# Attention's output kept by features, its squares read from PSUM: a hybrid diffusion layer on one core

## The chip, the core and the metric

One core of a Trainium2 chip runs the whole layer as one program. The metric is the device time of an execution in microseconds; "before" is the median of three runs. The core's engines each work through a queue of their own, in order: TensorE (PE, with its weight loads shown as PEld), VectorE (DVE), ScalarE (ACT), GpSimd (POOL), and SyncE (SP), which here only issues DMA transfers. They wait for one another by semaphores. TensorE writes its results into PSUM, a memory of eight banks, each with 512 fp32 columns on 128 partitions.

## The reference, cut to what matters

The layer serves 256 prompt tokens and 2048 latent tokens, width 1024. Its first half computes differential attention for four heads, and Fourier mixing beside it; both are joined by one output projection.

```python
s = einsum('bqhmd,bkhmd->bhmqk', q, k) * scale      # two maps m per head
p = softmax(s, axis=-1)
a = p[:, :, 0] - lam * p[:, :, 1]
o = einsum('bhqk,bkhe->bqhe', a, v)                 # 128 features e per head
...
a = rms_norm(o, subln_g) * (1.0 - lam_init)         # over the 128 features of a head
mix = concatenate([a.reshape(b, n, 512), four], axis=-1) @ w_out
```

The RMS norm of a head's output needs, for each query, the sum of squares over that head's 128 features, and one factor per query. Prompt tokens attend to themselves (256 keys), latent tokens to 512 cached and 2048 latent keys. A squared-ReLU MLP follows.

## The kernel before, in words

The kernel works in stages, one behind the other: modulation, input projection, Fourier mixing, attention, output projection with its norm, and two MLP stages that multiply by Strassen-like sums. The change touches attention and the output projection.

**Attention.** The work is cut into groups: 256 queries of one head make a group of two tiles (j = 0, 1), 8 groups a head, 32 in all, and one prompt group per head beside them. No loop order decides what runs when: every step of a group is entered in a list `ev` with a time in units of u (one unit is 5.2 / 5 us, five units make a step T), the list is sorted, and each engine's queue gets its instructions in that order. A step's time is thus a place in the queues, not a promise. A group takes 20 units. Seen from the start G of a group's period:

- The scores of a tile and a map (`fill`, L1080, 2 x 5 matmuls of 512 keys) go to five PSUM banks `S`; DVE takes their maxima (`rowmax`, L1085), ACT exponentiates them from there (`exp`, L1104, at 0, 5, 10 and 15 units, five each). The scores of the next map are written into the same five banks as they come free.
- POOL joins the two maps (`combine`, L1111 to L1120).
- PE transposes the result block by block (`tr`, L1135, two banks `pt`), ACT and DVE split it into a high and a low part (`ah` L1142, `al` L1147), and PE multiplies by the values (`mul`, L94 to L96, at 3.9, 8.9, 13.9 and 18.9 units; two of ten blocks in full precision, L1161). The products are summed in columns 0 to 255 of one bank, `po`, which holds features by queries: 128 features on the partitions, 256 queries.
- Behind a group's last product come the steps `o1` to `o6`: ACT copies the sum to SBUF (`oT`, L1172, 6 units into the next group's period), PE turns it into columns 256 to 511 of the same bank (`o2`, L1176, 6.4), DVE copies that out to `o` (`o3`, L1180, 10.25), ACT squares the copy with a running sum, one instruction for each tile (`o4`, L1186, 14.5), DVE adds epsilon (`o5`, L1189, 15.2) and POOL takes the power -1/2 (L91), POOL scales `o` and SP stores it (`o6`, L1195 and L1196, 15.6) as queries by features into `att`.

The bank `po` is shared: the prompt group's scores, and its products (`mul`, L1246, in two calls at 15.4 and 17.0 units), also lie in its columns 256 to 511, at times when no sample group's output is there. Its `o3` (L1250) copies them out; its `o4` to `o6` come about a group later.

For the last group the steps behind `o1` are not in the list but in `LASTO`, which the output projection interleaves with its first matmuls; their store runs on POOL's queue.

**Output projection.** 18 tiles of 128 tokens, each 2 x 24 matmuls (`out_mm`). Per tile SP loads `att` (L1560) and the Fourier half (L1562, by features already); `mix` has PE turn the attention half (L1572, four transposes), ACT copy it out with the gain (L1573), and DVE split it into high and low parts (L1576, L1577). Tile 0 is turned within the attention stage (`mix0_tr`, `mix0_copy`, L1280 and L1283). The output weights are split on the way in (`w_split`, L1544 and L1545).

Of the kernel before, what the change touches and what calls it, by code (L numbers as in the profile page):

```python
# [41 lines left out]
def body(tc, a, out):  # L42
    nc = tc.nc
    ctx = ExitStack()
    with ctx:
# [16 lines left out]
        att = [scratch(f"att{i}", [P, 512]) for i in range(NT // P)]  # L62
# [46 lines left out]
        def setup_cond(pool, pps, rows):  # L109
# [8 lines left out]
            nc.vector.tensor_scalar_mul(cols[:, 96:97], cols[:, 96:97], 1.0 - LAM_INIT)  # L118
# [870 lines left out]
        with ExitStack() as c3_:  # L989
# [49 lines left out]
            class Group:  # L1039
# [66 lines left out]
                def combine(self, j):  # L1106
# [5 lines left out]
                    nc.gpsimd.tensor_scalar(self.s0e[:, j:j + 1], tot[:, 0:1], tot[:, 0:1], EPS, op0=ALU.mult, op1=ALU.mult)  # L1112
# [65 lines left out]
                def o3(self):  # L1178
                    self.o = self.op.tile([P, 256], F32, tag="o", name=f"o{self.nm}")
                    nc.vector.tensor_copy(self.o, self.po[:, 256:512])  # L1180

                def o4(self):
                    osq = self.op.tile([P, P], F32, tag="osq", name=f"osq{self.nm}", bufs=1)
                    self.oss = self.op.tile([P, 4], F32, tag="oss", name=f"oss{self.nm}")
                    for j in range(2):
                        nc.scalar.activation(osq, self.o[:, j * P:j * P + P], AF.Square, accum_out=self.oss[:, j:j + 1])  # L1186

                def o5(self):
                    nc.vector.scalar_tensor_tensor(self.oss[:, 0:2], self.oss[:, 0:2], 1.0 / P, self.s0e, op0=ALU.mult, op1=ALU.add)  # L1189
                    pow_mhalf(self.oss[:, 2:4], self.oss[:, 0:2], 2)  # L1190

                def o6(self):
                    for j in range(2):
                        c = slice(j * P, j * P + P)
                        nc.gpsimd.tensor_scalar(self.o[:, c], self.o[:, c], self.oss[:, 2 + j:3 + j], 0.0, op0=ALU.mult, op1=ALU.add)  # L1195
                        (nc.gpsimd if self.last else nc.sync).dma_start(att[self.hd.tok0 + self.g * 2 + j][:, self.hd.hc], self.o[:, c])  # L1196

            class Prompt(Group):
# [21 lines left out]
                def combine(self, j):  # L1220
# [3 lines left out]
                    nc.gpsimd.tensor_scalar(self.s0e[:, j:j + 1], t[:, 2:3], t[:, 2:3], EPS, op0=ALU.mult, op1=ALU.mult)  # L1224
# [13 lines left out]
                def mul(self, j):  # L1238

                    (ah, al), V = self.A[0], self.hd.V  # L1240
                    n = 0
                    for t in range(2):
                        c = slice((t * 2 + j) * P, (t * 2 + j) * P + P)
                        for l, r in ((ah[:, c], V[:, t, 0, :]), (ah[:, c], V[:, t, 1, :]), (al[:, c], V[:, t, 0, :])):
                            n += 1
                            nc.tensor.matmul(PRO()[:, 256 + j * P:256 + j * P + P], l, r, start=False, stop=(n == 6), skip_group_check=True)  # L1246

                def o3(self):
                    self.o = self.op.tile([P, 256], F32, tag="o", name=f"o{self.nm}")
                    nc.vector.tensor_copy(self.o, PRO()[:, 256:512])  # L1250


# [8 lines left out]
            def load_wout():  # L1261
# [9 lines left out]
                MIX0.extend((f32(ts[0])[:, 2 * D:2 * D + 512], f32(ts[2])[:, 4 * D:5 * D].rearrange("p (k t) -> p k t", t=P)))  # L1271
                nc.sync.dma_start(MIX0[1][:, 4:8, :], four[:, 0:P].rearrange("(k p) t -> p k t", p=P))

            def mix0_load():
                nc.sync.dma_start(MIX0[0], att[0])

            def mix0_tr(gr):
                MIX0.append(gr.bank("pmx0", "pt"))
                for k in range(4):
                    nc.tensor.transpose(MIX0[2][:, k * P:k * P + P], MIX0[0][:, k * P:k * P + P], ident)  # L1280

            def mix0_copy():
# [849 lines left out]
```

## Time and profile before

| what | before |
|---|---|
| runs, median (lowest to highest) | 2862.73 us (2862.22 to 2862.76) |
| the profiled execution, span from the first to the last instruction | 2861.4 us |
| mean granted TensorE clock | 0.999 |
| DVE / ACT / POOL busy, whole span | 71% / 54% / 38% |
| DMA, mean | 172 GB/s |

Three kinds of lines are used below. A line of the timeline gives the start of an instruction, or of several alike in a row, in microseconds from the span's start, then the microseconds to the end of the last of them, engine, line of the kernel, operation, what it writes and reads, shapes, and a count; a bracket at the end is the idle time of that engine just before and who ended it. A line of groups gives a count behind the shape, and behind the bar the busy time, the mean duration in ns, and the idle time before. A line of the waits reads: who waited, for whom, microseconds in total, how often, the longest. A matmul's end is that of its pipeline: the next one starts before it, so that the step from start to start is what it costs PE.

### The profile page before, as it was taken

How to read it: one execution, taken by the hardware profiler on the slowest of the kernel's cores; microseconds unless marked ns; L12 is line 12 of the kernel's file. 1: busy time of each engine (PE TensorE's matmuls, PEld its weight loads, DVE VectorE, ACT ScalarE, POOL GpSimd, SP SyncE). 2: the span in 40 equal slices, each digit the busy share in tenths (PEclk: the TensorE clock that was granted, in tenths of full speed). 3: DMA queues.
4: the chain of work that ended last, by engine and by line, in shares of the span. 5: the costliest groups of instructions: out<-in, count | busy, mean ns of one | idle time of the engine just before them, and what ended most of it. 6: DMA issues, size and time to landing. Idle time of an engine off the chain costs nothing.

```text
span 2861.4 us, 43224 instructions
## 1 busy us (share of the span) xinstructions
PE 2831.7 (99%) x15109; PEld 2455.9 (86%) x15109; DVE 2018.0 (71%) x3393; ACT 1548.2 (54%) x3505; POOL 1073.3 (38%) x890
## 2 busy tenths in 40 slices
PE   8999999999999999999999999999999999999999
PEld 5888888688888888888889999999998888888887
DVE  7767886898988989864477777778775354345554
ACT  4333323798989989853356565556555332333221
POOL 1211223798999989942223333333332000000000
PEclk9999999999999999999999999999999999999999
DMA  7776777421211212036767676667747464445663
GB/s 284 219 207 198 230 213 237 172 106 38 73 71 53 106 38 99 23 124 201 242 221 232 223 246 228 221 219 238 234 167 255 147 202 135 138 144 185 206 206 111
DMA packets 392780, 492.94 MB, mean 172 GB/s; under 512 B 26467, under 2 KB 306384, under 8 KB 389490
## 3 DMA queue, kind: packets, MB, share of 16 engines
q1 hardware_dynamic: 387136, 479.73, 50.9%
q0 software_dynamic: 1872, 7.28, 0.8%
q10 hardware_dynamic: 3554, 3.17, 0.4%
q8 instruction: 119, 1.95, 0.3%
q14 instruction: 99, 0.81, 0.1%
HBM read 312.58 MB, written 179.59 MB: 172 GB/s over the span
## 4 chain that ended last, share of the span: by engine, by line
PE 54%; DVE 1%; DMA 0%; ACT 0%; issue 0%; SPq 0%; POOL 0%; DVEq 0%; POOLq 0%
PE ps L94 8%; PE ps L95 8%; PE ps L96 8%; PE pB L1749 2%; PE pB L1747 2%; PE pB L1748 2%; PE pA L1748 2%; PE pC L1748 2%; PE pA L1749 2%; PE pC L1747 2%; PE pA L1747 2%; PE pC L1749 2%; PE po L94 2%; PE po L96 2%; PE po L95 2%; PE pD L1749 1%
## 5 line engine op out<-in xcount | busy, mean ns | idle before, releaser
L1085 DVE TENSOR_REDUCE mxs<-Ss 128x1 f32<-128x512 f32 x636 | 405.4, 686 | 65.5 <-PE Ss L1080 55.1
L1420 DVE TENSOR_TENSOR sl<-sr,sh 128x768 fp32r<-128x768 f32 x168 | 161.8, 964 | 331.5 <-ACT sh L1419 331.1
L1120 POOL TENSOR_TENSOR P0s<-P0s,P1s 128x1024 f32<-128x1024 f32 (+2 forms) x128 | 378.6, 2958 | 10.7
L1419 ACT CAST sh<-sr 128x768 fp32r<-128x768 f32 x168 | 140.6, 838 | 418.3 <-PE ps L95 418.3
L1789 POOL TENSOR_TENSOR gs<-g,g 128x384 f32<-128x384 f32 x48 | 69.7, 1452 | 468.5 <-ACT g L1759 418.9
L1104 ACT ACTIVATE P1s<-Ss,mxs 128x512 f32<-128x512 f32 x318 | 215.4, 694 | 36.3 <-DVE mxs L1088 35.3
L94 PE MATMUL pj<-wh,hh 128*128 128x512 f32 x576 | 228.8, 397 | 2.0 <-DVE hh L555 2.0
L94 PE MATMUL ps<-thT,sh 128*128 128x512 f32 x585 | 227.6, 389 | 0.0
L95 PE MATMUL ps<-tlT,sh 128*128 128x512 f32 x585 | 227.6, 389 | 0.0
L96 PE MATMUL ps<-thT,sl 128*128 128x512 f32 x585 | 227.6, 389 | 0.0
L95 PE MATMUL pj<-wl,hh 128*128 128x512 f32 x576 | 227.1, 394 | 0.5 <-DVE wl L516 0.5
L96 PE MATMUL pj<-wh,hl 128*128 128x512 f32 x576 | 225.6, 392 | 0.0
L1104 ACT ACTIVATE P0s<-Ss,mxs 128x512 f32<-128x512 f32 x318 | 214.3, 691 | 5.6 <-DVE mxs L1088 5.0
L1135 PE MATMUL pts<-ident,P0s 128*128 128x128 f32 x1280 | 191.7, 273 | 4.5 <-DVE als L1147 1.8
L1080 PE MATMUL Ss<-KS0s,Qs 128*128 128x512 f32 x636 | 190.1, 419 | 0.4 <-ACT P1s L1104 0.4
L1080 PE MATMUL Ss<-KS1s,Qs 128*128 128x512 f32 x636 | 188.7, 420 | 1.5 <-ACT P0s L1104 1.4
L1758 ACT ACTIVATE g<-uz 128x384 f32<-128x384 f32 x144 | 75.7, 526 | 200.2 <-DVE uz L1781 174.1
L1135 PEld LDWEIGHTS pts<-ident,P0s 128*128 128x128 f32 x1280 | 151.3, 140 | 35.9 <-issue 4.8
L1119 POOL TENSOR_SCALAR P1s<-P1s,tots 128x1024 f32<-128x1024 f32 (+2 forms) x128 | 171.9, 1343 | 5.8
L1147 DVE TENSOR_TENSOR als<-pts,ahs 128x512 fp32r<-128x512 f32 x256 | 165.9, 681 | 6.9 <-ACT ahs L1142 6.7
L94 PE MATMUL ps<-ophT,sh 128*128 128x512 f32 x423 | 164.7, 389 | 1.1 <-DVE uz L1781 1.1
L96 PE MATMUL ps<-ophT,sl 128*128 128x512 f32 x423 | 164.6, 389 | 0.0
(536 smaller groups left out, 8073.9 us busy)
## 6 DMA issues: line engine op xcount, KB each, us to landing
sr<-sd SPq DMA_DIRECT2D x84, 768.0 KB, 4.5
a<-in_w SPq DMA_DIRECT2D x184, 256.0 KB, 4.2
sd<-gs SPq DMA_DIRECT2D x192, 192.0 KB, 1.9
sd<-g SPq DMA_DIRECT2D x144, 192.0 KB, 2.1
wm<-in_w_mod SPq DMA_DIRECT2D x32, 512.0 KB, 5.2
Qs<-qd SPq DMA_DIRECT2D x32, 512.0 KB, 4.0
b<-in_w SPq DMA_DIRECT2D x64, 256.0 KB, 5.8
b<-tsum SPq DMA_DIRECT2D x64, 256.0 KB, 4.7
```

The lines of the kernel that those rows point to most:

```text
L94: nc.tensor.matmul(ps, lh, rh, start=first, stop=False)
L95: nc.tensor.matmul(ps, lh, rl, start=False, stop=False)
L96: nc.tensor.matmul(ps, ll, rh, start=False, stop=last)
L1080: nc.tensor.matmul(S[:, :w], self.Q[:, x, m, j * P:j * P + P], self.hd.KS[m][:, b * 512:b * 512 + w], start=(x == 0), stop=(x == 1))
L1085: nc.vector.tensor_reduce(self.mx[j][:, m, b:b + 1], self.S[j, m, b], axis=AX.X, op=ALU.max)
L1104: nc.scalar.activation(dst, S, AF.Exp, bias=self.mx[j][:, m, 6:7], accum_out=self.sm[j][:, m, b:b + 1])
L1119: nc.gpsimd.tensor_scalar(p, p, tot[:, 3:4], 0.0, op0=ALU.mult, op1=ALU.add)
L1120: nc.gpsimd.tensor_add(d, d, p)
L1135: nc.tensor.transpose(pt[:, c:c + P], self.p0[j][:, (kb + t) * P:(kb + t + 1) * P], ident)
L1747: nc.tensor.matmul(ps, wh[:, c], hh[:, k, :], start=first and k == 0, stop=False, skip_group_check=True)
L1748: nc.tensor.matmul(ps, wh[:, c], hl[:, k, :], start=False, stop=False, skip_group_check=True)
L1749: nc.tensor.matmul(ps, wl[:, c], hh[:, k, :], start=False, stop=k == 3, skip_group_check=True)
```

## The change

It does six things. The output stays as features by queries (`oT`), and that is what is scaled and stored; the turned form stays in PSUM and serves the sums of squares alone, which ACT reads there (`o4`), so `o3` and the tile `o` are gone. Epsilon is added on POOL instead of DVE, and the division by 128 moves into epsilon and into the gain. The 256 factors of a group, which lie on the partitions of the queries, are stored to DRAM (`o6`) and loaded back broadcast over all partitions (`o7`); POOL multiplies (`o8`), and one store writes the group (`o9`). The prompt's product has V as the stationary operand, so it comes out by features too, and gets a turn in a `pt` bank of its own. In the projection, `mix_load` loads the attention half by features, the four transposes and ACT's copy go, and the gain moves into the first four blocks of the output weights.

```diff
-        att = [scratch(f"att{i}", [P, 512]) for i in range(NT // P)]
+        att = [scratch(f"att{i}", [512, 2 * P]) for i in range(NT // 256)]
+        rsd = [scratch(f"rs{h}", [NT // 256, 256]) for h in range(H)]
...
                 def o1(self):
-                    self.oT = self.op.tile([P, 256], F32, tag="oT", name=f"oT{self.nm}", bufs=1 if self.last else 2)
+                    self.oT = self.op.tile([P, 256], F32, tag="oT", name=f"oT{self.nm}", bufs=1 if self.last else 3)
...
-                def o3(self):
-                    self.o = self.op.tile([P, 256], F32, tag="o", name=f"o{self.nm}")
-                    nc.vector.tensor_copy(self.o, self.po[:, 256:512])
                 def o4(self):
...
-                        nc.scalar.activation(osq, self.o[:, j * P:j * P + P], AF.Square, accum_out=self.oss[:, j:j + 1])
+                        nc.scalar.activation(osq, self.po[:, 256 + j * P:256 + j * P + P], AF.Square, accum_out=self.oss[:, j:j + 1])
                 def o5(self):
-                    nc.vector.scalar_tensor_tensor(self.oss[:, 0:2], self.oss[:, 0:2], 1.0 / P, self.s0e, op0=ALU.mult, op1=ALU.add)
+                    nc.gpsimd.tensor_add(self.oss[:, 0:2], self.oss[:, 0:2], self.s0e)
                     pow_mhalf(self.oss[:, 2:4], self.oss[:, 0:2], 2)
+                def place(self):
+                    return nc.gpsimd if self.last else nc.sync, self.hd.tok0 // 2 + self.g
                 def o6(self):
-                    for j in range(2):
-                        c = slice(j * P, j * P + P)
-                        nc.gpsimd.tensor_scalar(self.o[:, c], self.o[:, c], self.oss[:, 2 + j:3 + j], 0.0, op0=ALU.mult, op1=ALU.add)
-                        (nc.gpsimd if self.last else nc.sync).dma_start(att[self.hd.tok0 + self.g * 2 + j][:, self.hd.hc], self.o[:, c])
+                    q, n = self.place()
+                    q.dma_start(rsd[self.hd.h][n].rearrange("(p j) -> p j", j=2), self.oss[:, 2:4])
+                def o7(self):
+                    q, n = self.place()
+                    self.rb = self.op.tile([P, 256], F32, tag="P0_1" if self.hd.s else "rb", ...)
+                    q.dma_start(self.rb, rsd[self.hd.h][n:n + 1].partition_broadcast(P).rearrange("p o d -> p (o d)"))
+                def o8(self):
+                    v = self.oT.rearrange("p (j t) -> p j t", j=2)
+                    nc.gpsimd.tensor_mul(v, v, self.rb.rearrange("p (t j) -> p j t", j=2))
+                def o9(self):
+                    q, n = self.place()
+                    q.dma_start(att[n][self.hd.hc], self.oT)
...
+                        for n, (l, r) in enumerate(((0, ah), (1, ah), (0, al))):        # Prompt.mul
+                            nc.tensor.matmul(PRO()[:, 256:512], V[:, t, l, :], r[:, c], ...)
...
-                for t, fn, *args in (... (15.4, gp.mul, 0), (17.0, gp.mul, 1),
-                                     (20.85, gp.o3), (39.5, gp.o4), (40.2, gp.o5), (40.6, gp.o6)):
+                for t, fn, *args in (... (17.0, gp.mul), (20.85, gp.o1), (24.2, gp.o2),
+                                     (24.9, gp.o4), (25.6, gp.o5), (28.2, gp.o6), (32.7, gp.o7),
+                                     (40.2, gp.o8), (43.0, gp.o9)):
...
-                    for t, fn in ((0, gr.o1), (0.4, gr.o2), (0.75 if gr.last else 4.25, gr.o3), (8.5, gr.o4), (9.2, gr.o5), (9.6, gr.o6)):
-                        if gr.last and t:
+                    for t, fn in ((0, gr.o1), (0.4, gr.o2), (8.5, gr.o4), (9.2, gr.o5), (11.8, gr.o6), (16.3, gr.o7), (23.4, gr.o8), (26.0, gr.o9)):
+                        if gr.last and t > 1:
...
-                    nc.scalar.copy(wh[k], WOUT[k][:, c])
-                    nc.vector.tensor_sub(wl[k], WOUT[k][:, c], f32(wh[k]))
+                    if k < H:
+                        nc.scalar.activation(wh[k], WOUT[k][:, c], AF.Copy, scale=cols[:, 96:97])
+                        nc.vector.scalar_tensor_tensor(wl[k], WOUT[k][:, c], cols[:, 96:97], f32(wh[k]), op0=ALU.mult, op1=ALU.subtract)
...
             def mix_load(i):
-                nc.sync.dma_start(am, att[i])
+                nc.sync.dma_start(mT[:, 0:4, :], att[i // 2][:, c:c + P].rearrange("(k p) t -> p k t", p=P))
...
-                    for k in range(4):
-                        nc.tensor.transpose(pm[:, k, :], am[:, k * P:k * P + P], ident)
-                    nc.scalar.activation(mT[:, 0:4, :], pm, AF.Copy, scale=cols[:, 96:97])
```

In the list the times of the prompt's steps count from the start of the head's sixth group period, so 24.2 is 4.2 units into the seventh. The times of the sample groups' `o` steps count from 6 units into the period that follows the group's products: 8.5 is at 14.5.

More of the change, by code (lines that the diff above doesn't have):

```diff
@@ L1236, in al, with mul, o1, o2 @@
                     self.A[0].append(t)
-                def mul(self, j):
+                def mul(self):
                     (ah, al), V = self.A[0], self.hd.V
-                    n = 0
                     for t in range(2):
[L1243 to L1250, printed above, removed]
+                        c = slice(t * 256, t * 256 + 256)
+                        for n, (l, r) in enumerate(((0, ah), (1, ah), (0, al))):
+                            nc.tensor.matmul(PRO()[:, 256:512], V[:, t, l, :], r[:, c], start=False, stop=(t == 1 and n == 2), skip_group_check=True)
+                def o1(self):
+                    self.oT = f32(at.tile([P, 512], F32R, tag="ahp", name=f"oT{self.nm}", bufs=1))[:, 0:256]
+                    nc.scalar.copy(self.oT, PRO()[:, 256:512])
+                def o2(self):
+                    self.pt[1] = pT.tile([P, 512], F32, tag="pt", name=f"pt{self.nm}_o")[:, 0:256]
+                    for j in range(2):
+                        nc.tensor.transpose(self.pt[1][:, j * P:j * P + P], self.oT[:, j * P:j * P + P], ident)
+                def o4(self):
+                    osq = at.tile([P, P], F32, tag="osq", name=f"osq{self.nm}", bufs=1)
+                    self.oss = at.tile([P, 4], F32, tag="oss", name=f"oss{self.nm}")
+                    for j in range(2):
+                        nc.scalar.activation(osq, self.pt[1][:, j * P:j * P + P], AF.Square, accum_out=self.oss[:, j:j + 1])
             ev = []
```

42 lines of the change are left out of this document (17 added, 25 removed).

## The prediction

> **What bounds the kernel now.** I read the page first, then the busy time by stretches, then who waited for whom in the attention stage, then PE's and ACT's instructions in order of time. The page says whose time the span is:
>
> ```profile
> span 2861.4 us, 43224 instructions
> PE 2831.7 (99%) x15109; PEld 2455.9 (86%) x15109; DVE 2018.0 (71%) x3393; ACT 1548.2 (54%) x3505; POOL 1073.3 (38%) x890
> ```
>
> The stretches show that this holds in both stages which the change touches: the first lies in attention, the second in the output projection. Columns: PE, PEld, DVE, ACT, POOL busy, granted clock, DMA share, GB/s.
>
> ```profile
> 900.00:1000.00 100.00, 100.00 (x651) 85.22 (x649) 89.78 (x179) 91.68 (x256) 92.51 (x74) 1.00 0.26 94
> 1300.00:1400.00 100.00, 100.00 (x491) 83.81 (x490) 49.49 (x65) 37.11 (x88) 27.73 (x25) 1.00 0.65 205
> ```
>
> So an instruction taken from PE is time won, one taken from DVE or ACT is not, and whatever makes PE wait is time lost. In attention the other engines stand at about 90%, so the question there is whether PE still finds its inputs ready. It is closest to ACT: the score matmuls write into five PSUM banks, and each bank is free only when ACT has exponentiated the scores before.
>
> ```profile
> PEld Ss L1080 <- ACT P0s L1104: 16.9, 52, 0.4
> ```
>
> Those 52 waits of PE's weight loads are short, 0.4 us at the longest; PE runs directly behind ACT. An ACT that comes two microseconds late is felt by PE at once.
>
> **Part one: the transposes that go.** In the projection, each tile of the mixed output had four transposes (L1572), and tile 0 had four in attention (L1280).
>
> ```profile
> L1572 PE MATMUL po<-ident,am 128*128 128x128 f32 x68 | 10.2, 272 | 0.0
> L1280 PE MATMUL pmx<-ident,wout 128*128 128x128 f32 x4 | 0.6, 272 | 0.0
> ```
>
> The busy column counts the tail of the pipeline; what they cost is the step from one start to the next:
>
> ```profile
> 1350.70 0.39 PE L96 MATMUL po<-woh,ml 128*128 128x512 f32 x1
> 1350.93 0.60 PE L1572 MATMUL po<-ident,am 128*128 128x128 f32 x4
> 1351.37 1.04 PE L248 MATMUL ptb<-ident,xn 128*128 128x128 f32 x8
> ```
>
> 1351.37 - 1350.93 = 0.44 us for four; 72 / 4 = 18 sets, so **-7.9 us**. ACT's copy of them and the DVE cast behind it start earlier; neither is on the path. In their place the load must be there: it takes the form of the load of the Fourier half, and is issued a whole tile ahead.
>
> ```profile
> mT<-four SPq DMA_DIRECT2D x17, 256.0 KB, 3.4
> att<-os SPq DMA_DIRECT2D x62, 64.0 KB, 1.6
> ```
>
> A tile takes 2 x 24 matmuls of 0.23 us (1350.70 to 1350.93), over 11 us, against 3.4 us to landing: hidden. If it were not, the term would be gone.
>
> **Part two: the prompt's product.** Twelve 128-wide matmuls in two calls become six 256-wide ones, plus two transposes.
>
> ```profile
> 1209.48 0.33 PE L1246 MATMUL po<-Vp,ahp 128*128 128x128 f32 x2
> ...
> 1210.09 0.68 PE L1080 MATMUL Ss<-KS0s,Qs 128*128 128x512 f32 x2
> ```
>
> One call cost 0.61 us, two 1.2. A 256-wide matmul steps by 0.11 us (1005.93 to 1006.04, quoted below), so six are 0.7; the transposes step by 0.1 each (0.44 / 4), together 0.2. That is -0.3 us for each of four heads, **-1.2 us**.
>
> **Part three: ScalarE reads the squares from PSUM.** This decides. Before, DVE copied the turned output out (o3), and ACT squared the copy (o4) at 8.5 units of the schedule behind o1. Now o4 keeps its place and reads the second half of bank po itself. The first half of that bank is the accumulator of the next group. In the event list, three products of the next group (13.9 units from its start, L1161 and L94 to L96) stand just ahead of o4 (14.5), and the five exponentials of the next scores (15.0 on) just behind it. Here is that place on PE and, below, on ACT:
>
> ```profile
> 1003.77 1.02 PE L1161 MATMUL po<-ahs,vf4s 128*128 128x256 f32 x4
> ...
> 1005.93 0.28 PE L96 MATMUL po<-ahs,Vs 128*128 128x256 f32 x1
> 1006.04 0.60 PE L1135 MATMUL pts<-ident,P0s 128*128 128x128 f32 x4
> 1006.40 1.63 PE L1080 MATMUL Ss<-KS0s,Qs 128*128 128x512 f32 x6
> ...
> 1009.25 0.60 PE L1135 MATMUL pts<-ident,P0s 128*128 128x128 f32 x4
> ```
>
> ```profile
> 1003.93 0.35 ACT L1186 ACTIVATE osqs<-os 128x128 f32<-128x128 f32 x1
> ...
> 1004.63 0.19 ACT L1186 ACTIVATION_READ_ACCUMULATOR osqs<-os 128x1 f32 x1
> 1005.08 0.69 ACT L1104 ACTIVATE P1s<-Ss,mxs 128x512 f32<-128x512 f32 x1 [0.27 <-DVE mxs L1088]
> ...
> 1005.76 0.68 ACT L1104 ACTIVATE P1s<-Ss,mxs 128x512 f32<-128x512 f32 x1
> ...
> 1009.88 0.59 ACT L1142 CAST ahs<-pts 128x512 fp32r<-128x512 f32 x1 [0.38 <-PE pts L1135]
> ```
>
> ACT starts its squares 0.16 us after PE starts the three products. Does a read of the second half wait for writes into the first? The trace shows the reverse case, a write into the first half that waits for a read of the second:
>
> ```profile
> 1237.49 1.10 PE L1161 MATMUL po<-ahs,vf4s 128*128 128x256 f32 x4 [0.56 <-DVE os L1180]
> 1236.92 0.42 DVE L1180 COPY os<-po 128x256 f32<-128x256 f32 x1 [0.72 <-DMA att<-os]
> ```
>
> PE's product goes to columns 0 to 255, DVE's copy reads 256 to 511, and still PE started only when the copy had ended (1236.92 + 0.42 = 1237.34). Order is kept by the bank, not by the column. I take it to hold for reads behind writes too. The Trainium skill says so outright (page "PSUM — Partial Sum Buffer", section "PSUM bank collisions raise a hardware error"): accesses of two engines to one bank and the same 32 partitions have to be kept apart by semaphores, whatever the addresses. By that rule the sum is the forecast; by addresses it would be the first rival below. The trace agrees for the one direction, with the 0.56 us; no row shows the other.
>
> Then o4 waits until the products end, 1005.93 + 0.28 = 1006.21. A wait of ACT on PE is over 0.03 us behind PE's end (1009.25 + 0.60 against 1009.88), and o4 takes 1004.63 + 0.19 - 1003.93 = 0.89. The exponentials start at 1007.13 instead of 1005.08, so the first bank is free at 1007.13 + 0.69 = 1007.82. PE wants it at 1006.40: **1.4 us idle**. Then the next two score products wait for exponentials that come every 0.68 us, while PE needs only 0.45 (two matmuls of 0.23): 0.2 us each, 0.4. A following stretch of the same group gives some back, since ACT is then late by a little less than PE, and the short waits quoted at the start go: -0.25 us, an estimate. About **1.65 us a group**; ends: 1.2 (the first wait less the rebate) and 2.0 (all waits, a 0.2 us hand-over, no rebate).
>
> ```profile
> L1186 ACT ACTIVATE osqs<-os x64: 309/312/358, 580.7 to 1248.9; 128x128 f32<-128x128 f32 x64
> ```
>
> 64 squares are 32 groups. The last three groups' squares have no exponentials behind them; 29 x 1.65 = **+47.9 us** (35 to 58).
>
> The prompt's squares get a true dependency as well: its transposes stand at 4.2 units of a group (behind three products, 3.9) and its o4 at 4.9, ahead of exponentials at 5.0.
>
> ```profile
> 862.42 0.60 PE L1135 MATMUL pts<-ident,P0s 128*128 128x128 f32 x4
> 862.77 0.71 PE L1080 MATMUL Ss<-KS0s,Qs 128*128 128x512 f32 x2
> 863.46 0.44 PE L1176 MATMUL po<-ident,oTs 128*128 128x128 f32 x2
> 861.69 0.69 ACT L1104 ACTIVATE P1s<-Ss,mxs 128x512 f32<-128x512 f32 x1 [0.99 <-DVE mxs L1088]
> ```
>
> PE reaches that place at 862.42 and needs 0.44 us (as the pair at 863.46); o4 then runs 862.9 to 863.8, and the exponentials that began at 861.69 begin 2.1 us later. Less what the inserted transposes take and a like rebate, PE loses 1.7 us a head: **+6.8 us** (3 to 8).
>
> **Part four: the rest.** The DVE copy that made PE wait in the drain goes: 0.56 us, twice, **-1.1**. In the drain o4 also waits for products, then the casts behind it and, at the seam, the last group's transposes are moved ahead, so that PE may wait for o1: **+2.0** (0 to 4), by the nearest wait there, the 0.56, and by o4's delay of 2.2 (1006.21 - 1003.93, rounded down). DVE loses o3 and o5 in every group; PE does not wait for DVE, so nothing. POOL swaps two scalings for one product of 128x256 and a small addition:
>
> ```profile
> L1195 POOL TENSOR_SCALAR os<-os,osss x64: 363/372/1367, 588.6 to 1254.5; 128x128 f32<-128x128 f32 x64
> 599.21 0.26 POOL L1224 TENSOR_SCALAR s0ep<-tlp 128x1 f32<-128x1 f32 x1
> 600.13 0.74 POOL L1226 TENSOR_TENSOR P0p<-P0p,P1p 128x256 f32<-128x256 f32 x1
> ```
>
> -2 x 0.37 + 0.74 + 0.26 (0.7 at most, nearer the small one since the addition has two elements a lane): +0.3 us a group of 22 us, where POOL idles 7.5%, 1.6 us. Hidden; if the cover were gone, the part beyond 1.6 us would be PE's. On SP, the store of the factors (o6) waits for POOL, and the broadcast load (o7) waits in the same queue until it has landed, 1.6 us by the row of the stores above; queued behind is the next group's query load, used three steps of 5.2 us later. o8 stands 11.6 units behind o6, and POOL has a whole combination of the next scores in between, so it finds the factors there. In the last group these run on POOL's queue in the projection, where POOL idles 72%. The scaling of the output weights changes an operand of eight casts and eight subtractions, not their number, and DVE idles half of that stage. None of this is on the path.
>
> **The sum.** -7.9 - 1.2 + 47.9 + 6.8 - 1.1 + 2.0 = +46.5 on the span of 2861.4: 2907.9. The median of the runs shown is 2862.73, 1.3 us above the span, so **2909 us**. Ends: -7.9 - 1.2 - 1.1 with 35 + 3 + 0 gives 2890, with 58 + 8 + 4 gives 2923.
>
> **Rivals.** (1) Not slower: reads are ordered by address, and only the prompt's squares wait. Then the 47.9 goes, and so does the drain's half of the 2.0: 2862.7 - 7.9 - 1.2 - 1.1 + 6.8 + 1 = 2860, no measurable change (0.2%, 5.7 us, is about what a measurement of this kernel tells from none). Against it stands PE's 0.56 us wait; for it, that no row shows a read waiting. It is decided by one thing: whether o4 starts before or after 1006.21 in such a group. (2) Faster: as (1), and PE gets to the prompt's transposes before ACT wants them, where the scheduler puts them ahead of the products. 2860 - 7 = 2853. For it: PE's transposes need only an early ACT copy. Against: elsewhere in the stage both queues follow the event list. (3) GpSimd becomes the bound, reads being ordered by address: if its product reads the interleaved factors so slowly that it costs 2.4 us more, 0.8 us a group is uncovered, 29 x 0.8 = 23: 2883. Point of decision: 1.6 us of added work. The 0.74 row speaks against it.
>
> **How the numbers follow.** Forecast 0.81; rival (1) 0.07, (2) 0.08, (3) 0.04. Ends of the forecast's terms rarely come together, so 2890 to 2923 leaves out little of the 0.81, and the rest lies below. Widened by a microsecond it is 2889 to 2924. Slower 0.85 (forecast and (3)), same 0.07, faster 0.08.
>
> **What would show it.** Right: ACT's squares preceded by an idle time of about 2 us released by PE's L96, and PE's score matmuls by about 1.4 us released by ACT, in 29 groups; PE's busy share in attention near 93%; period of a group from 22 to 23.7 us; the projection shorter by 7.5 us. Wrong: o4 running while L94 to L96 run, attention as long as before, or POOL as the releaser of PE.

## The result and the profile after

| | before | after |
|---|---|---|
| median (lowest to highest) | 2862.73 us (2862.22 to 2863.09) | 2910.35 us (2909.51 to 2911.3) |
| span of the profiled execution | 2861.4 us | 2907.7 us |
| attention, first to last full-precision product | 684.7 us | 737.8 us |
| from there to the end | 1618.2 us | 1613.1 us |
| ordinary group's period in attention | 22.0 us | 23.74 us |

An ordinary period, here and below, is the median over the samples' groups, from one turn of the output to the next in PE's timeline, without the three periods of a head that carry a prompt's products, turn and squares and without the drain, the last two.

The ratio of the times is 1.0168 (95% interval 1.0155 to 1.0180): slower, and 1.4 us from the forecast. The page of the kernel after shows that PE is still the engine of the span, with fewer matmuls (15021 for 15109) and yet 10 us more of busy time, since the tail of a row ahead of a wait and a wait inside a row (2.07 us for six matmuls, below) count as busy:

```profile
span 2907.7 us, 42986 instructions
PE 2841.9 (98%) x15021; PEld 2446.2 (84%) x15021; DVE 1983.5 (68%) x3321; ACT 1535.3 (53%) x3491; POOL 1074.3 (37%) x891
```

The same two stretches by engine as in the prediction (the second 50 us later): in attention every engine has become less busy at once, PE from 100.00 to 95.64, while in the projection PE is as busy as before.

```profile
900.00:1000.00 100.00, 95.64 (x601) 78.29 (x600) 80.99 (x157) 84.66 (x238) 84.87 (x68) 1.00 0.28 71
1350.00:1450.00 100.00, 100.00 (x479) 83.64 (x478) 47.62 (x70) 35.06 (x88) 25.71 (x26) 1.00 0.73 217
```

All engines less busy, none fuller: that is a longer chain of waits, not a heavier engine. To place it, cut the span at the first and the last full-precision product, in the timeline of PE. Before, first, with two neighbouring turns of the output (L1176), whose distance is a group's period:

```profile
558.50 0.38 PE L1161 MATMUL po<-ahs,vf4s 128*128 128x256 f32 x1
...
951.74 0.44 PE L1176 MATMUL po<-ident,oTs 128*128 128x128 f32 x2
973.79 0.44 PE L1176 MATMUL po<-ident,oTs 128*128 128x128 f32 x2
...
1243.20 0.28 PE L1161 MATMUL po<-ahs,vf14s 128*128 128x128 f32 x1
```

And after, with what lies between the three products and the next scores of one group (the lines are one or two further down in this kernel: products L95 to L97 and L1162, scores L1081, transposes L1136, turn L1177, squares L1183, exps L1105):

```profile
556.78 0.38 PE L1162 MATMUL po<-ahs,vf4s 128*128 128x256 f32 x1
...
812.31 0.44 PE L1177 MATMUL po<-ident,oTs 128*128 128x128 f32 x2
...
820.28 1.02 PE L1162 MATMUL po<-ahs,vf4s 128*128 128x256 f32 x4
...
822.39 0.28 PE L97 MATMUL po<-ahs,Vs 128*128 128x256 f32 x1
822.51 0.60 PE L1136 MATMUL pts<-ident,P0s 128*128 128x128 f32 x4
824.20 2.07 PE L1081 MATMUL Ss<-KS0s,Qs 128*128 128x512 f32 x6 [1.09 <-ACT P1s L1105]
...
836.03 0.44 PE L1177 MATMUL po<-ident,oTs 128*128 128x128 f32 x2
...
1294.59 0.28 PE L1162 MATMUL po<-ahs,vf14s 128*128 128x128 f32 x1
```

Attention grew by 737.8 - 684.7 = 53.1 us, what follows shrank by 5.1 (2861.4 - 1243.20 = 1618.2 against 2907.7 - 1294.59 = 1613.1), and the stages ahead were 1.7 shorter in this execution: 53.1 - 5.1 - 1.7 = 46.3, the whole difference of the spans. The change adds no work to the stages ahead, and over the profiled runs of this document, whatever the kernel, their end lies between 556.55 and 558.50 us, so the 1.7 are not put down to it. Within the group, the scores start 824.20 - 820.28 = 3.92 us behind the products; before it was 1006.40 - 1003.77 = 2.63. Six of them then take 2.07 us instead of 1.63. That is 1.29 + 0.44 = 1.73 us, and the periods shown grew from 22.05 to 836.03 - 812.31 = 23.72, by 1.67. ACT's timeline shows what they waited for, in the same group; the first lines are those of a prompt's squares:

```profile
687.67 1.10 ACT L1143 CAST ahs<-pts 128x512 fp32r<-128x512 f32 x2
691.22 0.28 ACT L1271 ACTIVATE osqp<-ptp_o 128x128 f32<-128x128 f32 x1 [2.45 <-issue]
...
819.51 1.09 ACT L1143 CAST ahs<-pts 128x512 fp32r<-128x512 f32 x2
822.71 0.28 ACT L1183 ACTIVATE osqs<-po 128x128 f32<-128x128 f32 x1 [2.11 <-PE po L97]
...
823.28 0.19 ACT L1183 ACTIVATION_READ_ACCUMULATOR osqs<-po 128x1 f32 x1
823.37 0.68 ACT L1105 ACTIVATE P1s<-Ss,mxs 128x512 f32<-128x512 f32 x1
```

ACT stands idle for 2.11 us, starts 0.04 us behind the end of the last product (822.39 + 0.28 = 822.67), and the exponentials start only behind the squares, at 823.37. They could have gone before: DVE had the last of their maxima at 821.50.

```profile
821.34 0.16 DVE L1089 TENSOR_REDUCE mxs<-mxs 128x1 f32<-128x5 f32 x1
```

The waits over all of attention say that it is so in 30 of the 32 groups (who, for whom, us in total, times, longest):

```profile
PEld Ss L1081 <- ACT P1s L1105: 68.6, 116, 1.5
ACT osqs L1183 <- PE po L97: 64.0, 30, 2.3
...
PE Ss L1081 <- ACT P1s L1105: 34.7, 32, 1.2
...
PEld Ss L1081 <- ACT P0s L1105: 14.9, 43, 0.5
...
ACT osqp L1271 <- issue: 9.1, 4, 2.5
```

Thirty waits of the squares on L97, 2.1 us each, four of the prompts' squares, and PE's score matmuls released by ACT. POOL releases PE nowhere.

### The profile page after: what moved, and what is told of

Its sections match the earlier page's. It is cut to its first block, busy times and chain, and to the rows that moved or that the text cites. A ratio compares the mean times of both kernels' runs of the same rounds, so it can differ in the third digit from the quotient of the medians.

```text
span 2907.7 us, 42986 instructions
## 1 busy us (share of the span) xinstructions
PE 2841.9 (98%) x15021; PEld 2446.2 (84%) x15021; DVE 1983.5 (68%) x3321; ACT 1535.3 (53%) x3491; POOL 1074.3 (37%) x891
## 4 chain that ended last, share of the span: by engine, by line
PE 53%; DVE 1%; DMA 0%; issue 0%; ACT 0%; POOL 0%; SPq 0%; DVEq 0%; POOLq 0%
PE ps L95 8%; PE ps L96 8%; PE ps L97 8%; PE pB L1755 2%; PE pB L1753 2%; PE pB L1754 2%; PE pA L1753 2%; PE pA L1754 2%; PE pC L1755 2%; PE pC L1753 2%; PE pA L1755 2%; PE pC L1754 2%; PE po L97 2%; PE po L95 2%; PE po L96 2%; PE pD L1755 1%
## 5 line engine op out<-in xcount | busy, mean ns | idle before, releaser
L1081 PE MATMUL Ss<-KS0s,Qs 128*128 128x512 f32 x636 | 201.6, 429 | 35.1 <-ACT P1s L1105 35.1
L95 PE MATMUL pj<-wh,hh 128*128 128x512 f32 x576 | 228.3, 396 | 2.3 <-DVE hh L556 2.0
L1105 ACT ACTIVATE P1s<-Ss,mxs 128x512 f32<-128x512 f32 x318 | 215.0, 696 | 25.5 <-DVE mxs L1089 24.5
L95 PE MATMUL ps<-thT,sh 128*128 128x512 f32 x585 | 227.6, 389 | 0.0
L97 PE MATMUL ps<-thT,sl 128*128 128x512 f32 x585 | 227.6, 389 | 0.0
L97 PE MATMUL pj<-wh,hl 128*128 128x512 f32 x576 | 225.5, 392 | 0.0
L1105 ACT ACTIVATE P0s<-Ss,mxs 128x512 f32<-128x512 f32 x318 | 214.3, 691 | 5.1 <-DVE mxs L1089 4.0
L1136 PE MATMUL pts<-ident,P0s 128*128 128x128 f32 x1280 | 191.6, 273 | 5.1 <-DVE als L1148 2.0
L1081 PE MATMUL Ss<-KS1s,Qs 128*128 128x512 f32 x636 | 187.9, 419 | 1.8 <-ACT P0s L1105 1.4
L1136 PEld LDWEIGHTS pts<-ident,P0s 128*128 128x128 f32 x1280 | 151.2, 140 | 36.9 <-issue 4.6
L1081 PEld LDWEIGHTS Ss<-KS0s,Qs 128*128 128x128 f32 x636 | 97.6, 189 | 82.9 <-ACT P1s L1105 71.4
L95 PE MATMUL ps<-ophT,sh 128*128 128x512 f32 x423 | 164.7, 389 | 1.1 <-DVE uz L1787 1.1
```

What stands on the lines that cost most here:

```text
L95: nc.tensor.matmul(ps, lh, rh, start=first, stop=False)
L97: nc.tensor.matmul(ps, ll, rh, start=False, stop=last)
L1081: nc.tensor.matmul(S[:, :w], self.Q[:, x, m, j * P:j * P + P], self.hd.KS[m][:, b * 512:b * 512 + w], start=(x == 0), stop=(x == 1))
L1105: nc.scalar.activation(dst, S, AF.Exp, bias=self.mx[j][:, m, 6:7], accum_out=self.sm[j][:, m, b:b + 1])
L1136: nc.tensor.transpose(pt[:, c:c + P], self.p0[j][:, (kb + t) * P:(kb + t + 1) * P], ident)
```

## The experiments

The theory was that the order kept between PE and ACT through the bank po is the cost; the rivals were the rest of the change (the factors' trip through DRAM, GpSimd's additions, the prompts). The first four runs take the two apart. Each run's ratio is to the kernel before in the same session; medians of different sessions differ by a microsecond or so for the kernel before itself (2862.15 to 2863.7), so a microsecond between runs of different sessions says nothing.

**before_psum: the suspected read alone, in the kernel before.** The copy and everything else stay; the last group still reads the copy.

```diff
-                        nc.scalar.activation(osq, self.o[:, j * P:j * P + P], AF.Square, ...)
+                        src = self.o[:, j * P:j * P + P] if self.po is None or self.last else self.po[:, 256 + j * P:256 + j * P + P]
+                        nc.scalar.activation(osq, src, AF.Square, ...)
```

> The kernel before, with one thing of the change: a sample's squares read the output from po in PSUM and no longer VectorE's copy in SBUF. The copy itself, the transposes, the POOL scaling and the stores all stay as before. Theory (the new dependency between the squares and the scores' products through the po bank is the whole cost): the ordinary group's period goes from about 22.0 to 23.7 us, ScalarE idles about 2 us ahead of the squares, behind the product at L97 or its counterpart, and the time is 2862.7 + 29 x 1.75 = about 2913 us, give or take 8. Rival (the cost comes from the rest of the change: the factors' trip through DRAM, GpSimd's epsilon and product, the prompts): the time stays within 5 us of 2862.7.

Measured: 2915.59 us, ratio 1.0181 (1.0166 to 1.0196), ordinary period 23.74. Its waits in attention (L1187 are the squares, L1080 the scores) are those of the changed kernel:

```profile
ACT osqs L1187 <- PE po L96: 64.2, 30, 2.5
...
PEld Ss L1080 <- ACT P1s L1104: 58.0, 104, 1.3
...
PE Ss L1080 <- ACT P1s L1104: 27.3, 25, 1.1
...
PE po L1247 <- ACT osqs L1187: 3.4, 4, 0.9
```

One operand, and the whole loss of an ordinary group is there; attention takes 735.3 us, 50.6 more than before. The rest of the change is not needed for it. That the whole times are so near to one another (2915.59 and 2910.35) is in part chance: here the prompts' products also wait for the squares whose columns they overwrite (the last row), and the projection still has its transposes.

**flip: the same two steps, the other way round.** Only the place of the squares in the event list changes, from behind the three products to just ahead of them.

```diff
-(8.5, gr.o4)
+(7.85, gr.o4)
```

> The changed kernel with a sample's squares listed at 7.85 in place of 8.5, just ahead of the three products into the same bank; ScalarE's own order and that of all other engines stays the same, and only the direction of the wait between the squares and the products turns round. Theory: TensorE now waits for ScalarE's two squares, which follow two casts, some 0.5 to 1.0 us in a group, and ScalarE's exps are no longer late: a period of about 22.5 to 23.0 us and a time of 2877 to 2892 us. Rival (GpSimd, the DMA trips or SyncE's queue set the longer period): nothing moves, 2905 to 2915 us.

Measured: 2895.43 us, ratio 1.0116 (1.0100 to 1.0131), period 23.13. The wait has turned round, and now PE's products wait for ACT:

```profile
PEld po L1162 <- ACT osqs L1183: 41.2, 31, 1.6
...
PE po L1162 <- ACT osqs L1183: 28.1, 31, 1.4
```

The direction and the mechanism are as expected, the price is not: 1.1 us a group where 0.5 to 1.0 was expected, and a time above the 2892 us named. The squares stand right behind two casts on ACT, and PE is there before ACT has done them. Products write columns 0 to 255 and squares read 256 to 511; each waits for the other, whichever stands first in the list.

**early: squares ahead of the casts.** 8.5 becomes 7.25, nothing else.

> The changed kernel with a sample's squares listed at 7.25 in place of 8.5, ahead of the two casts that stand before them on ScalarE; nothing else is moved. Theory: the squares start when ScalarE is free of its exps, are done before the products' turn, and neither side waits: the ordinary period falls back to about 22.0 us, 2856 to 2870 us in all; what is left of the change's cost is the prompts' share of about 3 us. Rival (GpSimd, DMA or SyncE): 2900 us or more. Second rival (the casts pushed back by 0.6 us stall the products that read them): 2875 to 2890 us.

Measured: 2866.97 us, ratio 1.0012 (1.0003 to 1.0021), period 22.18. What is left in the waits:

```profile
ACT osqp L1271 <- PE ptp_o L1265: 8.6, 4, 2.2
...
PEld po L1162 <- ACT osqs L1183: 9.9, 30, 0.3
```

So some 43 of the 47.6 us were an affair of one place in a list. The two rows show what is left of waits for squares: the four prompts, and 0.3 us of PE's weight loads in each group.

**copy_back: the changed kernel with DVE's copy again.**

```diff
+                def o3(self):
+                    self.o = self.op.tile([P, 256], mybir.dt.bfloat16, tag="osq", bufs=1, ...)
+                    nc.vector.tensor_copy(self.o, self.po[:, 256:512])
...
-                        nc.scalar.activation(osq, self.po[:, 256 + j * P:256 + j * P + P], AF.Square, ...)
+                        nc.scalar.activation(self.o[:, j * P:j * P + P], self.o[:, j * P:j * P + P], AF.Square, ...)
```

> The changed kernel with VectorE's copy put back at 4.25: a sample's squares read a copy of the turned output in SBUF, which is held in bfloat16 for room (the squares' inputs are rounded to it, and this is the only thing computed otherwise). The factors via DRAM, the GpSimd work, the features-by-queries output and the prompts' part stay as changed. Theory: with the dependency through po gone the period falls back to about 22.0 us and the time to 2856 to 2870 us. Rival (the cost lies in the rest of the change): 2900 us or more.

Measured: 2863.26 us, ratio 1.0000 (0.9990 to 1.0009), period 21.99. The four runs agree: with the read through the bank at that place the loss is there in either kernel, and without it, or with the read moved, an ordinary group is back at 22.0 to 22.2 us. GpSimd, the factors' trip and the layout cost nothing that shows in an ordinary period. Attention is 688.3 us, 3.6 more than before, and that is the prompts' squares: 0.9 us in each of four pairs of periods. DVE's copy, 32 small instructions on an engine with room, had kept ACT out of PE's bank.

**prompt_late: the second dependency.** On top of early, the prompts' squares go behind three exponentials and a copy.

```diff
-(24.9, gp.o4), (25.6, gp.o5)
+(26.5, gp.o4), (27.2, gp.o5)
```

> The changed kernel with a sample's squares at 7.25 as before this run, and the prompts' squares moved from 24.9 to 26.5 and the sum behind them from 25.6 to 27.2, three exps and a sample's copy later on ScalarE. In the run with 7.25 alone ScalarE stood for 2.1 to 2.2 us ahead of the prompts' squares in four groups, and those groups with the one behind each cost 1.2 to 1.6 us more than in the kernel before. Theory: these waits go, the four groups lose about 1.2 us each, and the time falls from 2867 to about 2862 us (2859 to 2865). Rival (TensorE's lateness in these groups comes from the twelve prompt products and not from ScalarE's wait): no change, 2865 to 2869 us.

Measured: 2864.34 us, ratio 1.0007 (0.9998 to 1.0016). The two periods that carry a prompt's turn and squares took 45.6 us together before, 50.0 after, 46.9 in early and 45.5 here (between the starts of the sample turns in PE's timeline, as above). Set against two ordinary periods of the same kernel, early's pair is 0.9 us a head above that of before, and here 0.4 below. The wait was ACT's place in the list once more, and with it gone the pair is shorter than before for the first time; the shorter prompt product is the likely reason, though no run has it alone. In time it brought 1.6 to 2.6 of the 5 us expected (against the kernel before of each session, and by the medians): attention fell from 693.8 to 687.0 us, but what follows grew from 1612.4 to 1617.2, which is the seam, below.

**both, gap, gap2: can the squares stay in PSUM and cost nothing?** All three are prompt_late with the squares at 6.55, 3.1 or 2.25; gap also has the edits of seam, below, whose own ordinary period is 22.15.

> As the run before, and a sample's squares one exp earlier still, at 6.55: with 7.25 TensorE's weight load still stood 0.3 us for the squares in 30 groups, and the ordinary period was 22.17 where the kernel before has 21.98 to 22.0. Theory: that wait goes, the period falls by 0.15 to 0.2 us in 29 groups, 4 to 6 us in all: about 2857 us (2853 to 2861), below the kernel before by the transposes that the change took out of the projection. Rival (the 0.17 us is the price of the squares' place on ScalarE, not of the wait): 2860 to 2864 us.

Measured: 2876.91 us, ratio 1.0051 (1.0039 to 1.0064), period 22.63. Neither the theory nor its rival: worse than at 7.25 by 12.6 us.

```profile
PEld Ss L1081 <- ACT P0s L1105: 37.8, 72, 0.8
...
PE Ss L1081 <- ACT P0s L1105: 10.4, 29, 0.4
```

The wait for squares is gone from the products, and the scores wait instead: the squares had pushed the last exponential of P0 back, and PE needs its bank.

> The run before with a sample's squares at 3.1 in place of 7.25: ahead of the third cast, where ScalarE stood 0.39 us for TensorE in each group. Theory (what is left of the 0.17 us in a group comes from 0.7 us of squares in a stretch of ScalarE's queue that has no room): the period falls to 22.0 to 22.05, 3 to 5 us below the run before, and TensorE waits for squares nowhere. Rival (the exps that follow are late by the 0.28 us that don't fit into the gap, and the scores wait for them): 0.1 to 0.3 us more in a group, 3 to 9 us above the run before.

Measured: 2925.29 us, ratio 1.0212 (1.0198 to 1.0226), period 23.92. The miss is instructive, for the mechanism of the theory was right and I had overlooked where it applies:

```profile
ACT osqs L1183 <- PE po L97: 43.5, 25, 1.8
...
PE Ss L1081 <- ACT P0s L1105: 39.5, 27, 1.7
```

3.1 behind o1 is 9.1 units into the period, and at 8.9 stand two other products into the same bank. The squares were once more just behind products, with a cast and exponentials behind them.

> The run with the prompts' squares at 26.5 (2864.3 us), with a sample's squares at 2.25 in place of 7.25: 8.25 units into the period, ahead of the products into the same bank at 8.9 and of the three casts that stand around them. The run at 3.1 (9.1 units) had set the squares behind those products, and ScalarE stood 1.8 us for them again. Theory (any place behind products into the bank costs, and any place ahead of them costs only ScalarE's 0.66 us where no gap takes it up): no wait of the squares for products, about 0.3 us of the 0.66 not covered ahead of the exps, so a period of 22.0 to 22.5 and 2860 to 2874 us. Rival (the 3.1 run was slow for its early place, not for the bank): again 23.9 us a group, 2915 us or more.

Measured: 2873.39 us, ratio 1.0037 (1.0023 to 1.0050), period 22.46, both at the upper end of what was expected. Ahead of those products the bank costs next to nothing (PE waits for squares once, 1.3 us), and the place costs ScalarE's own time, not through the exponentials but through the casts that PE's transposes need:

```profile
PE pts L1136 <- ACT ahs L1143: 10.8, 29, 0.4
```

Together, by place in the period (products into the bank at 8.9 and 13.9 units):

| squares at | 8.25 | 9.1 | 12.55 | 13.25 | 13.85 | 14.5 | copy in SBUF, 14.5 |
|---|---|---|---|---|---|---|---|
| period, us | 22.46 | 23.92 | 22.63 | 22.15 | 23.13 | 23.74 | 21.99 |

Of the places tried none reaches the copy's 21.99: right behind products costs 1.7 to 1.9 us, right ahead of them (13.85) 1.1, elsewhere 0.15 to 0.65, where the squares wait for no product and ACT's 0.66 us of squares stand in a stretch in which PE takes its outputs as they come. The copy (bfloat16 in copy_back, as its expectation says) can be squared at 14.5 units; from PSUM that very place is the worst but one.

**both_tr: the transposes' worth.** Four idle transposes per tile are put back into the projection of both (17 tiles), into the free bank.

```diff
+                if i != s0:
+                    for k in range(4):
+                        nc.tensor.transpose(PRO()[:, k * P:k * P + P], mT[:, k, :], ident)
```

> The run before with four idle transposes put back on TensorE ahead of each token tile's cast in the projection, 17 tiles, into the bank po, where nothing reads them: only the work of the transposes that the change took away, not the copy behind them nor the waits for it. Theory (the prediction's 18 x 0.44 us were TensorE's time): 17 x 0.44 = 7.5 us longer than the run before, 6 to 9. Rival (the transposes lay in gaps, and the gain came from elsewhere or not at all): within 2 us of the run before.

Measured: 2885.87 us, 9.0 more than both by the medians, 6.8 by the profiled spans. The group of the new transposes in its trace:

```profile
L1582 PE MATMUL po<-ident,mT 128*128 128x128 f32 x68 | 10.7, 281 | 3.0 <-DMA mT<-att 3.0
```

That is in the range of 6 to 9: the transposes were PE's time, as 17 x 0.44 = 7.5 says; the 3.0 us wait for a load at the first tile is not added, for in both PE stands 2.3 us for the cast of the same load.

**seam, copy_all, final: where the rest of that gain went.** In prompt_late PE stands 1.1 and 2.1 us at the start of the projection, for the casts of the first two tiles:

```profile
PE po L95 <- DVE mh L1582: 3.2, 2, 2.1
```

SP's queue shows why, and DVE's cast of the second tile behind it:

```profile
1239.98 0.37 SPq L1208 DMA_DIRECT2D att<-oTp  x1
1244.20 0.37 SPq L1295 DMA_DIRECT2D wout<-att  x1
...
1246.12 0.32 SPq L1194 DMA_DIRECT2D rs<-osss  x1
1250.02 0.32 SPq L1199 DMA_DIRECT2D rbs<-rs  x1
1250.45 0.37 SPq L1575 DMA_DIRECT2D mT<-att  x1
...
1256.45 0.69 DVE L1582 CAST mh<-mT 128x1024 fp32r<-128x1024 f32 x1 [2.40 <-DMA mT<-att]
```

The load of tile 0 (L1295) waits until the last prompt's output, issued at 1239.98, has landed. The load of the factors (L1199) waits in SP's queue until their store has landed, 3.9 us from issue to issue, and the second tile's loads stand behind it. The run seam puts the last but one group's transfers on GpSimd's queue and the last prompt's scaling earlier:

```diff
-return nc.gpsimd if self.last else nc.sync, ...
+return nc.gpsimd if self.last or self.hd.h == H - 1 and self.g == self.hd.ng - 2 and not self.hd.s else nc.sync, ...
...
-                    add(G[5] + t * u, fn, *args)
+                    add(G[5] + ({40.2: 37.0, 43.0: 38.5}.get(t, t) if h == H - 1 else t) * u, fn, *args)
```

> The run with a sample's squares at 7.25 and the prompts' at 26.5, and two edits to the queues at the seam to the projection: the factors' and output's transfers of the last but one group go through GpSimd's queue, as those of the last group do, and the last head's prompt scales and stores 4.5 and 3.2 steps earlier. There SyncE had stood 3.9 us behind the load of a row of factors that waited for its own store, with the projection's loads behind it; VectorE's casts came 2.4 us late twice, and TensorE stood 1.1 and 2.1 us for them. Theory (the factors' trip blocks SyncE, and at the seam nothing covers that): those waits go, 2 to 3.5 us less than 2864.3, so 2861 to 2862.5. Rival (the loads are late for the transfers' own time, not for SyncE's order): 2863 to 2866.

Measured: 2867.21 us, ratio 1.0013 (1.0005 to 1.0022), no better, and above the rival's range too. The two waits fell to one of 0.4 us, and another came:

```profile
PE ptb L249 <- DVE xn L236: 6.5, 1, 6.5
```

```profile
1268.29 0.54 POOL L1199 DMA_DIRECT2D rbs<-rs  x1 [3.17 <-DMA rs<-osss]
1273.97 0.72 POOL L1204 TENSOR_TENSOR oTs<-oTs,rbs 128x256 f32<-128x256 f32 x1 [5.14 <-DMA rbs<-rs]
...
1275.60 0.58 POOL L92 TENSOR_TENSOR nrsb<-nssb,mhalf 128x1 f32<-128x1 f32 x1
```

GpSimd is an in-order queue too: two trips one after the other on it held the power of the projection's first norm (L92) back, though DVE had its input ready at 1269.64, and PE stood 6.5 us for that norm. The block was moved, not removed.

The run copy_all has both edits of seam, the prompts at 26.5 and the copy of copy_back (not for the last group).

> The changed kernel with VectorE's copy for the squares put back (bfloat16, not for the last group), the prompts' squares at 26.5, and the two edits to the queues at the seam. Theory: the ordinary period is that of the kernel before, 22.0 us, the four prompts cost 0.3 us each, and the projection keeps the 5 to 7 us that the transposes took: 2862.6 - 5 to - 8 + 1 = 2855 to 2859 us, the shortest so far. Rival (with the factors' trip through DRAM the seam costs what the transposes gave): 2860 to 2864.

Measured: 2860.85 us, ratio 0.9994 (0.9985 to 1.0003), not to be told from the kernel before, and in the rival's range. Its attention takes 682.7 us, 2 less than before, but PE waits 4.0 us for the norm. The last run takes the GpSimd part back and has ACT issue the second tile's loads:

```diff
-                mix_load(s1)
...
                 w_split(1, 0, 1)
+                mix_load(s1, nc.scalar)
                 mix(s0)
```

> The run before with VectorE's copy (copy_all), with the last but one group's transfers on SyncE's queue again and the loads of the projection's second tile issued by ScalarE behind its first four weight casts. In copy_all GpSimd's queue, with two groups' transfers one after the other, held the first norm's power back, and TensorE stood 4.0 us for the norm where the kernel before stood 1.6. Theory (the trip of the factors costs at the seam through whichever in-order queue it blocks; here neither SyncE's nor GpSimd's block meets anything urgent): the 4.0 us fall to about 1, SyncE's wait no longer holds up the loads of the second tile, and the time is 2856 to 2859 us, below the kernel before. Rival (the issue on ScalarE delays its casts, or the loads land late all the same): 2860 us or more.

Measured: 2859.61 us, ratio 0.9985 (0.9976 to 0.9994): the only version whose interval lies below the kernel before, by 0.15%. It is 0.6 us above the range of the theory and 0.4 below the rival's, and the norm's wait, which was to fall to about 1 us, is 3.4. The intervals of copy_all and final overlap, so that the last step gained anything is not shown. The page and PE's waits from 1235 us on:

```profile
span 2854.6 us, 43141 instructions
```

```profile
PE ptb L249 <- DVE xn L236: 3.4, 1, 3.4
...
PE po L1177 <- ACT oTs L1173: 0.5, 1, 0.5
```

The waits for the second tile are gone. Of the 7.9 us of transposes some 4 arrive: from the last product to the end it takes 1614.2 us, before 1618.2; the profiled execution took 2856.36 us, 3.3 less than the median, so this is a little kind. A likely reason for the norm's wait is the gate's loads, which also stand behind the factors on SP (DVE waits for them twice, 4.5 us in all); no run takes it apart.

## Why the prediction was right

- **Samples' squares, +47.9 forecast.** Measured: 29 x (23.74 - 22.0) = 50.5 us. The mechanism is as described, and its parts differ a little. The first wait was put at 1.42 us with squares of 0.89; from PSUM they took 0.66 (822.71 to 823.37), and the scores were 1.29 late. The pacing by the exponentials was put at 0.4 and is 0.44. The rebate of 0.25 did not come: the short waits that were to go, 16.9 us in all before, are still 14.9. Two small errors against each other. Of the signs that were named, PE's busy share in attention was put near 93% and is 95.64%, since part of its waits counts as busy.
- **Order by bank or by column.** This was the fork, and the evidence was one drain row in which a write waited for a read of other columns. The 2.11 us in after are the direction that no row had shown, and the waits of up to 1.4 us in flip the other; rival (1), reads ordered by address, falls with the first, and rival (2), which builds on it, with it. By the rule of the Trainium skill (page "PSUM — Partial Sum Buffer", section "PSUM bank collisions raise a hardware error") two engines in one bank and the same 32 partitions must be kept apart whatever the addresses; the traces agree in both directions. What they show is a wait that the program sets by semaphore. The tile `po` fills its bank, so the runs don't tell order kept by bank from order kept by tile. Whether the chip would bear the overlap was not tried, since the wait can't be taken away alone.
- **Prompts, +6.8 and -1.2.** The four squares did wait, 9.1 us of ACT's time in all, but PE lost less by it: the pair of periods with a prompt's squares grew by 0.9 us a head beyond the samples' share, some 4 us for four (5.6 forecast). prompt_late takes the wait away: without it the pair is 0.4 us below that of before, so what is left, the product's gain if nothing else moved, is about -0.4 a head (-0.3 forecast), and the wait about +1.3 (1.7 forecast).
- **Transposes, -7.9, drain and seam, -1.1 and +2.0.** both_tr confirms the first by itself. Behind attention the change won 5.1 us where 7.5 had been named as a sign, and where 17 sets at 0.44 with the +2.0 give 5.5; in after, PE's waits at the seam are 0.46, 0.44 and 0.47 us. The drain's copy has no number of its own: from the drain's first turn to the last product PE took 20.9 us where before it took 22.8, and these -1.9 hold the copy, tile 0's transposes and whatever waits came in.
- **POOL hidden.** Right, and rival (3) falls. The addition took 0.20 us (0.26 in the row used for it) and the product 0.74 (as in its row), and copy_back runs with all of that work at a period of 21.99.
- **SP's o7, hidden.** Right in attention and wrong in size: the store of 256 factors took 3.7 us from issue to landing in after (median of 31), not the 1.6 of the row taken for it. It made no difference to the forecast, with PE's waits at the seam as small as above; in prompt_late and seam it was the next wait.
- **The sum.** The earlier stages' -1.7 was in no term, and looks like scatter; with 53.1 and -5.1 it makes 46.3 against 46.5. That the two agree to 0.2 us is luck: terms that were off by 1 to 3 us made up for one another, so the mechanism is better supported than the last digit.

## What to carry to other kernels

When a change lets one engine read where another writes, look at what the memory's order is kept by, here the bank (or the tile that fills it), and at which writes stand just ahead in the list and which urgent work just behind: a small copy off the path may be there to cut that link. Before giving such a change up, move the reading step along the list, which recovered 43 of 48 us here, and compare with the copy at the same place. A trip through DRAM inside an in-order queue cost nothing here as long as everything behind it had slack; at the end of a stage see what stands behind it, on each queue to which it could be moved.

## What the runs showed of the hardware

- ACT's squares of 128x128 took 277 ns from PSUM (all 64 within 5 ns) and 312 from SBUF. Of the Trainium skill, the page "Perfetto Trace Analysis", section "Optimizing Scalar/DVE Operations", puts ScalarE's overhead of data access in an instruction at about 93 ns on SBUF and 51 on PSUM, as busy time of the engine. The difference of 42 ns, an estimate from these two figures, is near to the 35 ns between the medians here.

```profile
L1183 ACT ACTIVATE osqs<-po x64: 277/277/282, 581.2 to 1298.2; 128x128 f32<-128x128 f32 x64
```

- A store of 256 factors (1 KB) to DRAM and the load that brings them back to all partitions (128 KB) took long: in prompt_late 3.9 us from the store's issue to the load's, and then 1255.01 - 1250.02 = 5.0 us from there to GpSimd's product. The stores of 64 KB in the kernel before landed in 1.6 us (median).
- The granted clock was 0.999 in before and after, 0.997 in seam and 0.994 in gap, in runs on another chip where the kernel before had 0.999 again. gap's period is 0.2 us above that of after; how much of that is the clock stays open.
